# A causal convolution's sums begun two iterations ahead, its pivot at tile 2, and the high parts of the second product ahead of the next silu

## The chip, the cores and the metric

The kernel runs on 1 core of one Trainium2 chip. The metric is device microseconds of one execution: 2212.9 us as the median of 3 runs (2212.4 to 2215.72). One more execution was profiled; all rows below come from it.

The engines are PE (matmuls), DVE and ACT (elementwise work), POOL (elementwise work that may not touch PSUM) and SP, which issues the loads.

## The reference

Two layers over 256 positions of 2048 channels in float32. Only the first sub-layer matters here, the convolution module:

```python
def conv_module(x, pw1_w, pw1_b, dw_w, dw_b, ln_g, ln_b, pw2_w, pw2_b):
    h = x @ pw1_w + pw1_b
    a, gate = jnp.split(h, 2, axis=-1)
    h = a * jax.nn.sigmoid(gate)
    h = lax.conv_general_dilated(...)   # causal, depthwise, width 31
    h = h + dw_b
    h = jax.nn.silu(layer_norm(h, ln_g, ln_b))
    return h @ pw2_w + pw2_b
```

Behind it come a residual with a layer norm, an MLP (2048 to 8192 and back), keys and values, a dilated attention and a second MLP. They are not touched.

## The kernel before

Channels lie on the partitions, so activations are 16 tiles of 128 x 256. Each float32 operand is split into a high part, which PE takes at full rate, and a low part: a product is hi x hi + hi x lo + lo x hi. Weights come in units of 128 x 1024 (`Weights`, L69). Each unit is loaded by SP, cast to its high part by ACT (L117) and reduced to its low part by DVE or POOL (L118). Six high and six low buffers exist, so ACT can cast a unit only when PE has done with the one six back; ACT's casts keep step with PE.

**The convolution module** runs in 16 iterations, one per tile i. PE multiplies the gate half and then the value half of tile i (`pw1`, L247 to L249, 48 matmuls each). ACT takes the sigmoid of the gate (L425). DVE adds the bias to the value half and multiplies (L436, or L433 for tiles 13 and 15): the gated input. DVE then convolves 14 of the tiles itself, one `scalar_tensor_tensor` per tap of width 31 (L482). Its taps are dealt to the iterations by `_plan`, which the change leaves alone. Tiles 13 and 15 are convolved on PE, by matmuls with shifted diagonals (L450), which ACT makes (L420).

A running sum of DVE lies in PSUM. There are three banks (named `o`, `s`, `s`) with two halves each, so six sums. Each tile's first sum starts with its bias: `begin(i)` has ACT write it (L472; L469 for the first tiles). For the layer norm, all tiles are shifted by a pivot, a mean that PE computes from tile 0 (`ln_pivot`, L283, L285). Tiles from `PIVOTED` on get the shift with their bias in `begin`; the earlier ones are shifted afterwards by POOL (L488). `conv_sums` squares a finished tile on ACT (L506) and adds it to two running sums on POOL (L510, L512).

PE and DVE run these iterations in the order in which they are written (`manual_schedule`); ACT and POOL are put in order by the framework's scheduler, which also sets the semaphores.

**The norm and the second product.** `ln_stats` finishes mean and variance. For each tile, DVE multiplies by the scale (L595), ACT takes the silu (L596), ACT casts the high part (L589) and DVE subtracts it for the low part (L590); this runs two tiles behind. PE multiplies with 16 blocks of the second weight (L267, L268), three blocks at once at first, so that each tile is used as it comes. Its last block uses L247 to L249, and the statistics of the next norm begin with L341.

Of the kernel before, what the change touches and what calls it, by code (L numbers as in the profile page):

```python
# [20 lines left out]
T = 256  # L21
D = 2048
KT = D // P
# [31 lines left out]
NGP = 4  # L55
DIAGS = (8192 - NGP * (PAD + T) - 4 * SEG) // 128 * 2
SPLIT = (0, 1, 2, 14)
PIVOTED = 3
STATS_AT = 12

PERIOD, PAIR, STALL, GLU, LATE, SOON = 29, 0.54, 1.34, 2.6, 2, 6
# [69 lines left out]
def trunk(ctx: ExitStack, tc, xt, vecs, dww, dwut, rbt, onehot, w_pw1, w_pw2, w_k, w_v, w_q, w_o, w_1, w_2, out):  # L131
    nc = tc.nc
# [15 lines left out]
    def bank(p, name):  # L148
        return p.tile([P, 512], F32, name=name)
# [130 lines left out]
    def ln_pivot(ln, z0):  # L280

        ps = bank(ps_t, "t")
        nc.tensor.matmul(out=ps[:, 0:T], lhsT=inv, rhs=z0, start=True, stop=True)  # L283
        npiv = small.tile([P, T], F32, name="npiv")
        nc.scalar.mul(out=npiv, in_=ps[:, 0:T], mul=-float(KT))  # L285
        ln["npiv"] = npiv
# [102 lines left out]
    def scale_residual(bias=None, of=range(KT)):  # L389
        for kt in of:  # L390
            y = xres[:, kt, :]
            if bias is None:
                nc.scalar.mul(out=y, in_=y, mul=ALPHA)
            else:
                nc.scalar.activation(out=y, in_=y, func=AF.Identity, scale=ALPHA, bias=vec[:, bias + kt:bias + kt + 1])
# [18 lines left out]
    def make_diags(n):  # L414

        nonlocal made
        for i, g, k in diags[made:min(made + n, taken + DIAGS)]:
            j = made % DIAGS
            with tc.issue_after(W.last_hi.ins):
                nc.scalar.activation(out=work[:, j * 64:(j + 1) * 64], in_=eye, func=AF.Copy, scale=dwu[:, i, g, k:k + 1])  # L420
            made += 1

    def glu(i, a, gate):
        sig = tmp.tile([P, T], F32, name="sig", tag="a")
        on_act = nc.scalar.activation(out=sig, in_=gate, func=AF.Sigmoid,  # L425
                                      bias=vec[:, V_PWB + KT + i:V_PWB + KT + i + 1])
        b = vec[:, V_PWB + i:V_PWB + i + 1]
        if i in PE_TILES:
            ph = ph_of[PE_TILES.index(i) % 2]
            for g in range(2):  # L430
                for s in range(2):
                    h = half(g)
                    nc.vector.scalar_tensor_tensor(out=ph[half(s), g, LAGS - 1:], in0=halves(a)[h, s], scalar=b[h],  # L433
                                                   in1=halves(sig)[h, s], op0=ALU.add, op1=ALU.mult)
        else:
            nc.vector.scalar_tensor_tensor(out=gp_of[DVE_TILES.index(i) % NGP][:, PAD:], in0=a, scalar=b, in1=sig,  # L436
                                           op0=ALU.add, op1=ALU.mult)
        return on_act

    def pe_conv(i, g, midway=None):  # L440

        nonlocal taken
        o = bank(ps_mm, "mm")[:, 0:P]
        ph = ph_of[PE_TILES.index(i) % 2]
        assert taken + 2 * LAGS <= made <= taken + DIAGS and DIAGS % 2 == 0
        for n in range(LAGS):
            if midway and n == STATS_AT:
                midway()
            j = taken % DIAGS
            nc.tensor.matmul(out=o, lhsT=work[:, j * 64:(j + 2) * 64], rhs=ph[:, g, LAGS - 1 - n:LAGS - 1 - n + P],  # L450
                             start=n == 0, stop=n == LAGS - 1)
            taken += 2
        return o
# [10 lines left out]
    def begin(i):  # L464

        if i in DVE_TILES:
            b = vec[:, V_DWB + i:V_DWB + i + 1]
            if i < PIVOTED:
                nc.scalar.activation(out=sum_of[i, 0], in_=inv[:, 0:1].to_broadcast([P, T]), func=AF.Identity, scale=0.0,  # L469
                                     bias=b)  # L470
            else:
                nc.scalar.activation(out=sum_of[i, 0], in_=ln["npiv"], func=AF.Identity, bias=b)  # L472
# [13 lines left out]
    def shift(i):  # L486
        z = conv[:, i, 0:T]
        nc.gpsimd.tensor_tensor(out=z, in0=z, in1=ln["npiv"], op=ALU.add)  # L488
# [16 lines left out]
    def conv_sums(i):  # L505
        nc.scalar.activation(out=conv[:, i, T:2 * T], in_=conv[:, i, 0:T], func=AF.Square)  # L506
        if i >= KT - 2:
            ln["last"].append((conv[:, i, 0:T], conv[:, i, T:2 * T]))
        elif i == 1:
            nc.gpsimd.tensor_tensor(out=ln["acc"], in0=conv[:, 0, :], in1=conv[:, 1, :], op=ALU.add)  # L510
        elif i:
            nc.gpsimd.tensor_tensor(out=ln["acc"], in0=ln["acc"], in1=conv[:, i, :], op=ALU.add)  # L512

    def pw1(units, outs):
        for kt in range(KT):
            h, k = divmod(kt, KT // 2)
            for (_, us), o in zip(units, outs):
                hi, lo = W.get(us[h])
                three(o, hi[:, k * P:(k + 1) * P], lo[:, k * P:(k + 1) * P], x_hl[:, kt, :], kt)

    ended = []

    def pe_convs(at):
        return [(i, g, pe_conv(i, g)) for i, g, when in PE_CONV[:-1] if when == at]

    def pe_ends(convs):
        for i, g, o in convs:
            pe_end(i, g, o)
            if g:
                ended.append(i)  # L530

    def taps(i):
        for *tap, ends in plan[i]:
            dve_tap(*tap, ends)
            if ends == 2:
                if tap[0] < PIVOTED and ln["npiv"] is not None:
                    shift(tap[0])
                ended.append(tap[0])

    begin(0)  # L540
    with tc.manual_schedule(engines={PE, DVE}):
        for i in range(KT):
            if i == 0:
                a, gate = (bank(ps_mm, "mm")[:, 0:T] for _ in range(2))
                pw1(u_pw1[0], (a, gate))
                convs = []
            else:
                acc = bank(ps_mm, "mm")
                a, gate = acc[:, 0:T], acc[:, T:2 * T]
                pw1(u_pw1[2 * i - 1], (gate,))  # L550
                if i == PIVOTED:
                    ln_pivot(ln, conv[:, 0, 0:T])
                    begin(i)
                    for j in ended:
                        shift(j)
                convs = pe_convs(i)
                pw1(u_pw1[2 * i], (a,))
            sigmoid = glu(i, a, gate)
            if i + 1 != PIVOTED:
                begin(i + 1)  # L560
            make_diags(math.ceil((len(diags) - made) / (KT - i)))
            if 4 <= i < 12:
                with tc.issue_after(W.last_hi.ins):
                    scale_residual(V_PW2B, (2 * i - 8, 2 * i - 7))
            pe_ends(convs)
            if i < KT - 1:
                taps(i)
            if i > PIVOTED:
                while ended[:-2] and ended[0] < KT - 2:
                    conv_sums(ended.pop(0))  # L570
        convs = pe_convs(KT)
        taps(KT - 1)
        pe_ends(convs[:-1])
        for j in ended:
            conv_sums(j)
        with tc.issue_after(sigmoid.ins):

            warm = small.tile([P, 1], F32, name="warm")
            nc.scalar.activation(out=warm, in_=inv[:, 0:1], func=AF.Silu)
        i, g, _ = PE_CONV[-1]  # L580
        pe_ends(convs[-1:] + [(i, g, pe_conv(i, g, lambda: ln_early(ln)))])
        conv_sums(KT - 1)
    conv_z = lambda kt: conv[:, kt, 0:T]
    rs = ln_stats(ln, conv_z, 3, u_pw2[0][0][1][0], WARM_C)
    s_hl = act.tile([P, KT, 512], F32R, name="act")

    def split_silu(kt):
        hi, v = s_hl[:, kt, 0:T], conv_z(kt)
        nc.scalar.copy(out=hi, in_=v)  # L589
        nc.vector.tensor_tensor(out=s_hl[:, kt, T:2 * T], in0=v, in1=hi.bitcast(F32), op=ALU.subtract)  # L590

    with tc.manual_schedule(engines={ACT, DVE}):
        for kt in range(KT):
            t = conv_z(kt)
            nc.vector.tensor_tensor(out=t, in0=t, in1=rs, op=ALU.mult)  # L595
            nc.scalar.activation(out=t, in_=t, func=AF.Silu, scale=vec[:, V_CG + kt:V_CG + kt + 1],  # L596
                                 bias=vec[:, V_CB + kt:V_CB + kt + 1])
            if kt >= 2:
                split_silu(kt - 2)
        for kt in (KT - 2, KT - 1):  # L600
            split_silu(kt)


    def residual(units, rhs, first, last, ln, bias=None):
# [81 lines left out]
    for c in range(4):  # L686
        accs = [bank(ps_mm, "mm") for _ in range(2)]
        for kt in range(KT):
            j, k = divmod(kt, 4)
            u = u_v[c][j][k // 2]  # L690
            hi, lo = W.get(u)
            hi, lo = hi[:, (k % 2) * 512:(k % 2 + 1) * 512], lo[:, (k % 2) * 512:(k % 2 + 1) * 512]
# [227 lines left out]
```

## Time and profile before

| what | value |
| --- | --- |
| median of 3 runs | 2212.9 us |
| profiled execution | 2216.65 us |
| its span | 2214.9 us |
| PE busy | 2164.5 us, 98% |
| DVE busy | 1417.5 us, 64% |
| ACT busy | 1037.8 us, 47% |
| POOL busy | 421.7 us, 19% |

The span runs from the first to the last instruction of the profiled execution. A matmul's record lasts longer than the time to the next one, since matmuls are pipelined, so PE counts as busy as long as they follow each other closely. The convolution module, with its second product and the norm behind it, takes roughly the first 360 us. The granted clock of PE has two levels, 1.2 and 2.4 GHz; a mean of 0.80 over a stretch means that part of it ran at the lower one.

### The profile page before, as it was taken

What the parts mean: (1) busy time and instruction counts of PE and PEld (TensorE: products, weight loads), DVE (VectorE), ACT (ScalarE), POOL (GpSimd) and SP (SyncE); (2) the same over time, 40 slices, a digit from 0 to 9 for tenths busy, and PEclk for the clock granted to TensorE, in tenths of its full rate; (3) what the DMA queues carried; (4) which work ended last, traced back from release to release, by engine and by line L of the source; (5) the groups of instructions that cost most, each with busy time, mean ns of one, the idle gap of its engine ahead of it and who ended that gap; (6) DMA issues with size and microseconds to landing.
All of it is one profiled execution on the core that took longest, in us unless ns stands there. A gap on an engine that the chain in (4) does not pass through costs nothing.

```text
span 2214.9 us, 33327 instructions
## 1 busy us (share of the span) xinstructions
PE 2164.5 (98%) x12851; PEld 1909.0 (86%) x12851; DVE 1417.5 (64%) x2218; ACT 1037.8 (47%) x1559; POOL 421.7 (19%) x337
## 2 busy tenths in 40 slices
PE   8997899999999999999999999999999999999997
PEld 8997788888888888888888888878888888888886
DVE  8789567655665665666744476677656656656664
ACT  6664445433543443444644455455434434434443
POOL 5996382000000000015300000640000000000064
PEclk9998899999999999999999999999999999999998
DMA  7553164556855555555465554536555555555552
GB/s 274 185 187 111 46 212 151 189 188 178 249 184 189 185 187 190 190 190 184 136 217 188 192 163 150 189 122 217 187 190 183 188 190 190 190 185 187 186 185 86
DMA packets 113264, 398.04 MB, mean 180 GB/s; under 512 B 12432, under 2 KB 16976, under 8 KB 113104
## 3 DMA queue, kind: packets, MB, share of 16 engines
q1 hardware_dynamic: 111040, 392.75, 53.4%
q10 hardware_dynamic: 2064, 3.15, 1.1%
q8 instruction: 101, 1.65, 0.3%
q14 instruction: 59, 0.48, 0.1%
HBM read 390.61 MB, written 5.24 MB: 179 GB/s over the span
## 4 chain that ended last, share of the span: by engine, by line
PE 92%; DVE 5%; issue 1%; ACT 1%; POOL 1%; DMA 0%; SPq 0%; DVEq 0%; POOLq 0%
PE mm L267 51%; PE mm L268 26%; PE mm L249 3%; PE mm L247 3%; PE mm L248 3%; DVE s L482 2%; PE mm L698 1%; PE mm L696 1%; PE mm L697 1%; DVE o L482 1%; PE mm L450 0%; DMA raw<-in_w_pw 0%; DVE xres L381 0%; POOL act L362 0%; DVE act L368 0%
## 5 line engine op out<-in xcount | busy, mean ns | idle before, releaser
L267 PE MATMUL mm<-act,whi 128*128 128x512 f32 x4928 | 1739.1, 398 | 11.4 <-DVE act L368 5.9
L268 PE MATMUL mm<-act,wlo 128*128 128x256 f32 x4928 | 1383.1, 281 | 1.9 <-POOL wlo L118 1.9
L117 ACT CAST whi<-raw 128x1024 fp32r<-128x1024 f32 (+1 forms) x740 | 770.5, 1045 | 964.0 <-PE mm L267 552.2
L118 DVE TENSOR_TENSOR wlo<-raw,whi 128x1024 fp32r<-128x1024 f32 (+1 forms) x676 | 835.5, 1238 | 590.8 <-ACT whi L117 569.0
L267 PEld LDWEIGHTS mm<-act,whi 128*128 128x128 f32 x4928 | 926.0, 188 | 237.4 <-DVE act L590 8.4
L268 PEld LDWEIGHTS mm<-act,wlo 128*128 128x128 f32 x4928 | 932.6, 189 | 3.5 <-POOL wlo L118 2.2
L618 POOL TENSOR_TENSOR xres<-xres,npiv 128x256 f32<-128x256 f32 x8 | 8.6, 1076 | 1591.2 <-ACT npiv L285 1591.2
L247 PE MATMUL mm<-act,whi 128*128 128x256 f32 x704 | 201.4, 286 | 6.2 <-ACT whi L117 6.2
L249 PE MATMUL mm<-act,wlo 128*128 128x256 f32 x704 | 200.3, 284 | 0.2 <-DVE wlo L118 0.2
L248 PE MATMUL mm<-act,whi 128*128 128x256 f32 x704 | 199.9, 284 | 0.0
L118 POOL TENSOR_TENSOR wlo<-raw,whi 128x1024 fp32r<-128x1024 f32 x64 | 153.0, 2416 | 49.8 <-ACT whi L117 48.3
L247 PEld LDWEIGHTS mm<-act,whi 128*128 128x128 f32 x704 | 135.6, 193 | 7.4 <-ACT whi L117 6.7
L249 PEld LDWEIGHTS mm<-act,wlo 128*128 128x128 f32 x704 | 135.5, 192 | 0.9 <-DVE wlo L118 0.9
L248 PEld LDWEIGHTS mm<-act,whi 128*128 128x128 f32 x704 | 135.7, 193 | 0.1
L482 DVE SCALAR_TENSOR_TENSOR s<-act,dw,s 128x256 f32<-128x256 f32 x266 | 117.6, 482 | 16.7 <-ACT s L472 16.4
L611 DVE TENSOR_TENSOR xres<-mm,xres 128x256 f32<-128x256 f32 x128 | 54.0, 423 | 89.9 <-PE mm L268 73.3
L300 POOL TENSOR_TENSOR ln_acc<-ln_acc,xres 128x256 f32<-128x256 f32 x56 | 80.6, 1440 | 93.5 <-DVE xres L613 93.5
L482 DVE SCALAR_TENSOR_TENSOR o<-act,dw,o 128x256 f32<-128x256 f32 x150 | 72.2, 481 | 2.0 <-ACT o L472 1.4
L613 DVE TENSOR_TENSOR xres<-mm,xres 128x256 f32<-128x256 f32 x156 | 66.1, 424 | 5.1
L296 ACT ACTIVATE sq<-xres 128x256 f32<-128x256 f32 x60 | 25.1, 419 | 80.8 <-DVE xres L613 25.8
L625 POOL TENSOR_TENSOR xres<-xres,npiv 128x256 f32<-128x256 f32 x56 | 56.6, 1039 | 0.0
L234 DVE TENSOR_TENSOR act<-v,act 128x256 fp32r<-128x256 f32 x120 | 50.2, 419 | 6.6 <-ACT act L233 6.6
(146 smaller groups left out, 1120.6 us busy)
## 6 DMA issues: line engine op xcount, KB each, us to landing
raw<-in_w SPq DMA_DIRECT2D x512, 512.0 KB, 4.0
raw<-in_w_pw SPq DMA_DIRECT2D x94, 512.0 KB, 4.0
raw<-in_w_v SPq DMA_DIRECT2D x32, 512.0 KB, 4.3
raw<-in_w_k SPq DMA_DIRECT2D x32, 512.0 KB, 4.4
raw<-in_w_q SPq DMA_DIRECT2D x32, 512.0 KB, 4.3
raw<-in_w_o SPq DMA_DIRECT2D x32, 512.0 KB, 4.4
scratch<-es ACTq DMA_DIRECT2D x1, 3072.0 KB, 35.1
bt<-scratch SPq DMA_DIRECT2D x16, 128.0 KB, 4.1
```

What stands on the lines that cost most here:

```text
L117: self.last_hi = self.nc.scalar.copy(out=hi[:, s], in_=r[:, s])
L118: self.lo_engine[i].tensor_tensor(out=lo[:, s], in0=r[:, s], in1=hi[:, s].bitcast(F32), op=ALU.subtract)
L247: nc.tensor.matmul(out=o, lhsT=hi, rhs=x[:, 0:T], start=kt == 0, stop=False)
L248: nc.tensor.matmul(out=o, lhsT=hi, rhs=x[:, T:2 * T], start=False, stop=False)
L249: nc.tensor.matmul(out=o, lhsT=lo, rhs=x[:, 0:T], start=False, stop=kt == KT - 1)
L267: nc.tensor.matmul(out=acc, lhsT=hi, rhs=x, start=kt == 0, stop=kt == KT - 1)
L268: W.last_mm = nc.tensor.matmul(out=acc[:, T:2 * T], lhsT=lo, rhs=x[:, 0:T], start=False, stop=kt == KT - 1, skip_group_check=True)
L300: nc.gpsimd.tensor_tensor(out=acc[:, 0:T], in0=acc[:, 0:T], in1=z, op=ALU.add)
L482: nc.vector.scalar_tensor_tensor(out=out, in0=tap, scalar=w, in1=o, op0=ALU.mult, op1=ALU.add)
L611: nc.vector.tensor_tensor(out=y, in0=acc[:, 0:T], in1=y, op=ALU.add)
L613: nc.vector.tensor_tensor(out=y, in0=acc[:, T:2 * T], in1=y, op=ALU.add)
L625: nc.gpsimd.tensor_tensor(out=xres[:, b, :], in0=xres[:, b, :], in1=ln["npiv"], op=ALU.add)
```

## The change

Three things change. `PIVOTED` goes from 3 to 2, so PE computes the pivot in iteration 2, and tiles 0 and 1 alone are shifted afterwards. In iteration i the sum of tile i + 2 is begun, where it was that of tile i + 1. A finished tile waits for one more finished tile before its squares are taken. In the silu loop the cast of tile k - 2 (`silu_hi`) is written ahead of the silu of tile k, and the subtraction (`silu_lo`) stays where it was. No instruction of another form is added.

```diff
-PIVOTED = 3
+PIVOTED = 2
...
-    begin(0)
+    for i in range(PIVOTED):
+        begin(i)
...
                 if i == PIVOTED:
                     ln_pivot(ln, conv[:, 0, 0:T])
                     begin(i)
+                    begin(i + 1)
                     for j in ended:
                         shift(j)
...
             sigmoid = glu(i, a, gate)
-            if i + 1 != PIVOTED:
-                begin(i + 1)
+            if i >= PIVOTED:
+                begin(i + 2)
...
             if i > PIVOTED:
-                while ended[:-2] and ended[0] < KT - 2:
+                while ended[:-3] and ended[0] < KT - 2:
                     conv_sums(ended.pop(0))
...
-    def split_silu(kt):
+    def silu_hi(kt):
+        nc.scalar.copy(out=s_hl[:, kt, 0:T], in_=conv_z(kt))
+
+    def silu_lo(kt):
         hi, v = s_hl[:, kt, 0:T], conv_z(kt)
-        nc.scalar.copy(out=hi, in_=v)
         nc.vector.tensor_tensor(out=s_hl[:, kt, T:2 * T], in0=v, in1=hi.bitcast(F32), op=ALU.subtract)
...
         for kt in range(KT):
             t = conv_z(kt)
+            if kt >= 2:
+                silu_hi(kt - 2)
             nc.vector.tensor_tensor(out=t, in0=t, in1=rs, op=ALU.mult)
             nc.scalar.activation(out=t, in_=t, func=AF.Silu, scale=vec[:, V_CG + kt:V_CG + kt + 1],
                                  bias=vec[:, V_CB + kt:V_CB + kt + 1])
             if kt >= 2:
-                split_silu(kt - 2)
+                silu_lo(kt - 2)
         for kt in (KT - 2, KT - 1):
-            split_silu(kt)
+            silu_hi(kt)
+            silu_lo(kt)
```

Line numbers below 540 are the same in both; the silu's lines L589, L590, L595 and L596 of before are L590, L594, L601 and L602 of the changed kernel.

**ACT, iteration 6.** Before: L425 is the sigmoid of tile 6, L117 are casts of weight units, L395 scales the residual, and the last row is the begin of tile 7.

```order
L395 ACTIVATE xres_94<-xres_94,vec_112 128x256
L425 ACTIVATE sig_1486<-mm_1365,vec_112 128x256
L395 ACTIVATE xres_94<-xres_94,vec_112 128x256
L117 CAST whi_1533<-raw_1366 128x1024
L117 CAST whi_1563<-raw_1396 128x1024
L117 CAST whi_1593<-raw_1426 128x1024
L472 ACTIVATE s_191<-npiv_768,vec_112 128x256
```

The same place on ACT now; L472 here is the begin of tile 8.

```order
L117 CAST whi_1456<-raw_1289 128x1024
L420 ACTIVATE act_182<-eye_129,dwu_114 128x64 x8
L395 ACTIVATE xres_94<-xres_94,vec_112 128x256
L425 ACTIVATE sig_1484<-mm_1363,vec_112 128x256
L395 ACTIVATE xres_94<-xres_94,vec_112 128x256
L472 ACTIVATE s_192<-npiv_606,vec_112 128x256
L117 CAST whi_1531<-raw_1364 128x1024
```

The begin of iteration 6 stood three casts behind the sigmoid; it now stands ahead of these casts.

**POOL, the first shift.** Before, from the first low part of a weight unit on POOL; L488 is the shift of tile 0, then of tile 1.

```order
L118 TENSOR_TENSOR wlo<-raw,whi 128x1024 x12
L488 TENSOR_TENSOR act<-act,npiv 128x256
L118 TENSOR_TENSOR wlo<-raw,whi 128x1024 x2
L488 TENSOR_TENSOR act<-act,npiv 128x256
L118 TENSOR_TENSOR wlo<-raw,whi 128x1024
L510 TENSOR_TENSOR ln_acc<-act 128x512
```

The same place on POOL now.

```order
L118 TENSOR_TENSOR wlo<-raw,whi 128x1024 x8
L488 TENSOR_TENSOR act<-act,npiv 128x256
L118 TENSOR_TENSOR wlo<-raw,whi 128x1024 x4
L488 TENSOR_TENSOR act<-act,npiv 128x256
L118 TENSOR_TENSOR wlo<-raw,whi 128x1024 x2
L510 TENSOR_TENSOR ln_acc<-act 128x512
```

Eight low parts instead of twelve stand ahead of the first shift.

**ACT, the silu loop.** Before, from the mean's copy on: L596 is a silu, L589 the cast of the tile two back.

```order
L347 COPY ln_mc<-o 128x256
L596 ACTIVATE act<-act,vec 128x256 x3
L589 CAST act<-act 128x256
L596 ACTIVATE act<-act,vec 128x256
L589 CAST act<-act 128x256
```

The same place on ACT now, with L602 for the silu and L590 for the cast.

```order
L347 COPY ln_mc<-o 128x256
L602 ACTIVATE act<-act,vec 128x256 x2
L590 CAST act<-act 128x256
L602 ACTIVATE act<-act,vec 128x256
L590 CAST act<-act 128x256
```

Each cast moved ahead of one silu; DVE's order in this loop (a multiply, a subtraction two tiles back) is the old one but for two subtractions of weight units that moved out of it.

## Rows read from the trace of the kernel before

**Rows 1.** Windows: busy us (instructions) of each engine, granted clock, DMA share, GB/s.

```profile
180.00:232.00 52.00, 36.04 (x263) 35.58 (x262) 48.21 (x125) 19.35 (x49) 23.18 (x14) 0.80 0.22 74
...
240.00:274.00 34.00, 28.61 (x125) 22.35 (x126) 16.93 (x33) 17.17 (x34) 10.59 (x10) 0.85 0.19 62
...
340.00:360.00 20.00, 16.88 (x95) 13.31 (x96) 15.58 (x32) 8.73 (x17) 10.80 (x14) 1.00 0.14 49
```

**Rows 2.** Waits to 500 us: who waited for whom, us in total, times, longest.

```profile
DVE s L482 <- ACT s L472: 16.4, 4, 7.0
PE mm L450 <- DVE act L433: 16.0, 2, 8.6
...
PE mm L267 <- DVE act L590: 5.2, 8, 2.1
...
ACT s L472 <- DVE s L482: 4.7, 1, 4.7
...
PE mm L268 <- POOL wlo L118: 1.9, 1, 1.9
...
DVE o L482 <- ACT o L472: 1.4, 1, 1.4
```

**Rows 3.** Timeline of DVE: start, us, line, operation, tiles; in brackets idle before.

```profile
39.33 0.42 DVE L484 TENSOR_TENSOR act<-o,act 128x256 f32<-128x256 f32 x1
...
50.24 0.47 DVE L436 SCALAR_TENSOR_TENSOR act<-mm,vec,sig 128x256 f32<-128x256 f32 x1
...
70.29 0.49 DVE L482 SCALAR_TENSOR_TENSOR s<-act,dw,s 128x256 f32<-128x256 f32 x1 [7.04 <-ACT s L472]
...
81.63 0.48 DVE L436 SCALAR_TENSOR_TENSOR act<-mm,vec,sig 128x256 f32<-128x256 f32 x1
...
93.25 0.48 DVE L436 SCALAR_TENSOR_TENSOR act<-mm,vec,sig 128x256 f32<-128x256 f32 x1
...
104.35 0.47 DVE L436 SCALAR_TENSOR_TENSOR act<-mm,vec,sig 128x256 f32<-128x256 f32 x1
```

**Rows 4.** Timeline of PE, from the pivot to the next norm.

```profile
49.90 0.59 PE L283 MATMUL t<-act,inv 128*128 128x256 f32 x2
...
196.10 6.52 PE L450 MATMUL mm<-act 128*128 128x128 f32 x32 [7.37 <-DVE act L433]
...
220.53 8.93 PE L450 MATMUL mm<-act 128*128 128x128 f32 x56 [8.59 <-DVE act L433]
...
239.96 0.50 PE L267 MATMUL mm<-act,whi 128*128 128x512 f32 x1 [2.10 <-DVE act L590]
...
271.08 0.39 PE L267 MATMUL mm<-act,whi 128*128 128x512 f32 x1
...
271.43 0.39 PE L267 MATMUL mm<-act,whi 128*128 128x512 f32 x1
...
344.32 0.61 PE L341 MATMUL mm<-inv,xres 128*128 128x1 f32 x4
```

**Rows 5.** Timeline of ACT in the iterations; the casts are the 37th and the 41st.

```profile
77.32 0.47 ACT L472 ACTIVATE s<-npiv,vec 128x256 f32<-128x256 f32 x1
...
87.89 1.05 ACT L117 CAST whi<-raw 128x1024 fp32r<-128x1024 f32 x1 [1.83 <-PE mm L248]
...
99.41 1.05 ACT L117 CAST whi<-raw 128x1024 fp32r<-128x1024 f32 x1 [1.82 <-PE mm L248]
...
103.05 0.50 ACT L395 ACTIVATE xres<-xres,vec 128x256 f32<-128x256 f32 x1
```

**Rows 6.** Timeline of POOL: the low parts ahead of the first shift.

```profile
28.78 26.12 POOL L118 TENSOR_TENSOR wlo<-raw,whi 128x1024 fp32r<-128x1024 f32 x11 [0.27 <-ACT whi L117]
```

**Rows 7.** Timeline of ACT in the silu loop.

```profile
246.52 0.60 ACT L596 ACTIVATE act<-act,vec 128x256 f32<-128x256 f32 x1 [0.82 <-DVE act L595]
247.03 0.39 ACT L589 CAST act<-act 128x256 fp32r<-128x256 f32 x1
248.24 0.60 ACT L596 ACTIVATE act<-act,vec 128x256 f32<-128x256 f32 x1 [0.83 <-DVE act L595]
```

## The prediction

> **What bounds the kernel now.** I read the windows first, then the waits, then the timelines of DVE, ACT and PE in the stretches that they name. PE is the engine that ends the work, so only time that PE loses counts, and in the first 360 us it loses it in two places. From 180 to 232 us PE is busy 36.04 of 52 us and its granted clock averages 0.80; from 240 to 274 us it is busy 28.61 of 34 at 0.85 [rows 1]. The waits name the causes: PE waited 16.0 us, in two pieces, for L433, DVE's gated input of the two tiles that PE convolves, and 7.1 us (5.2 and 1.9) at the start of the second product for the low parts of the silu (L590) and of a weight unit [rows 2].
>
> Behind the first place stands DVE. It stood idle 17.8 us in five pieces (16.4 and 1.4) for L472, the activation by which ACT starts a sum with its bias [rows 2]; the longest is the 7.04 us ahead of 70.29 [rows 3]. Apart from these pieces DVE works without a gap until the convolution ends, and PE waits for it there at 196.10 (7.37 us) and before 220.53 (8.6 us) [rows 2, 4]. So each microsecond that DVE doesn't idle brings the end of the convolution forward by one, as long as DVE stays behind PE.
>
> **The sums (begin, pivot).** A sum is half a PSUM bank. The tap that waits for L472 is not one of the tile just begun: by the built order it writes the *other* half of that bank, for a tile two or three older. So each begin is a meeting: DVE stops at its next tap on that bank until ACT has come to the begin. Beginning earlier doesn't take the meeting away; it matters where ACT stands by then.
>
> The Trainium skill says in "PSUM — Partial Sum Buffer", section "PSUM bank collisions raise a hardware error", that two engines must be kept apart by bank and quadrant, not by address. By that rule the meeting stays and the term below is 12.3; were the wait by address, all 17.8 would go. The order agrees with the rule.
>
> Where ACT stands I count in casts of weight units (L117), which ACT can only do as PE frees buffers: the 37th at 87.89 and the 41st at 99.41 give 11.52 us for four, one iteration [rows 5]. Up to each begin, before and now: iteration 4, 33 and 33; iteration 5, 39 and 37; 6, 44 and 41; 7, 49 and 46; 8, 53 and 51; 9, 58 and 55. So the meetings come up to three casts (8.6 us) earlier. They also come later in DVE's own row: 2 taps behind the gated input of iterations 4 and 5, then 6, 11, 18 and 23. What is left to wait:
> - Iteration 2. The square of tile 0 stands on ACT ahead of a begin, a cast, eight diagonals, a cast and the sigmoid of tile 2, and waits for tile 0's shift on POOL, now behind 8 low-part subtractions instead of 12. These take 26.12/11 = 2.37 us, so the shift starts at 28.78 + 7 x 2.37 = 45.4 and ends near 46.2 [rows 6]. A cast, eight diagonals, a scaling and a sigmoid took 99.41 to 103.05 = 3.64 us [rows 5]; with the square, the begin and the other cast I estimate 5.0, so the gated input is free to go at 51.3 against 50.24 before [rows 3]: 1.1 us.
> - Iteration 4. DVE would come to its gated input at 81.63 - 7.04 + 1.1 = 75.7 [rows 3], two taps later it is 76.5. The begin stands right behind the 33rd cast, where a begin stood before at 77.32, and ends at 77.8 [rows 5]. Wait 1.3.
> - Iteration 5. 93.25 - 7.04 + 2.4 = 88.6, and two taps: 89.4. The begin stands behind the 37th cast and seven diagonals (1.7, an estimate from the same 3.64): 91.0. Wait 1.6.
> - Iteration 6. 104.35 - 7.04 + 4.0 = 101.3, and six taps of 0.39: 103.7. The begin follows the scaling at 103.05: 103.9. Wait 0.2.
> - From iteration 7 on the begin is three casts ahead of where it was and DVE comes 11 or more taps (4.3 us) later to it: nothing.
>
> That is 4.2 us. The pivot's matmul now asks for tile 0 after the gate of tile 2. PE gets there one iteration before 49.90, at 38.4 [rows 4], and tile 0 is done at 39.33 + 0.42 [rows 3]: PE waits 1.4 us, and the casts with it. With that on the meetings I take 5.5 us: the term is 17.8 - 5.5 = **-12.3**. Its bounds are -17.8 (no meeting waits) and, if ACT falls behind again, 0.
>
> Is DVE still the late one? PE's gate of tile 15 ended at 196.10 - 7.37 = 188.7. With two groups of 32 matmuls at 6.52 (the row, part of it at half clock), half an iteration of 5.76 and the 1.4, PE comes to tile 15's taps at 208.9 at the latest; at full clock, with groups near half as long, near 203. DVE would have its input by 220.53 - 12.3 = 208.2 [rows 4]. So PE still waits, or just doesn't, and the 12.3 holds. The squares a tile later cost nothing: ACT has room between its casts, and the last sums on POOL end ahead of the early statistics. One shift less on POOL is off the path.
>
> **The silu.** A tile took 1.72 us: Silu at 246.52, cast of its high part at 247.03, DVE's subtraction, DVE's multiply for the next tile, next Silu at 248.24 [rows 7]. All four stand in one ring, because the subtraction for tile k-2 comes on DVE ahead of the multiply for k+1 and its cast came behind the Silu of k. With the cast ahead of the Silu the ring spans two tiles: the same 1.72 us for two, 0.86 each. ACT alone needs 0.51 for a Silu and about 0.3 for a cast, 0.8 a tile. PE takes three blocks a tile, each 271.43 - 271.08 = 0.35, so 1.05 [rows 4]. PE becomes the slower one, and the 7.1 us of waits go.
>
> The stage as a check: from PE's first L267 at 239.96 to the last statistics at 344.32 it took 104.4 us [rows 4]. The work is 15 blocks x 16 x 0.35 = 84, a last block of 48 matmuls at 0.12 (11.52 over the 96 of an iteration) = 5.8, and some 2 for pivot and statistics: 92. The other 12 are the 7.1 of waits and the half-clock stretches between them: 0.15 x 34 = 5.1 at most [rows 1]. A dense start leaves no reason for these. I take **-10**, keeping 2 for the first tiles and for casts of later units that stand in ACT's order between the Silus. Bounds: -12.5 and -3 (the rate is hidden behind something else, as the 1.9 for a late weight unit was).
>
> **Sum.** -12.3 - 10 = -22.3. The profiled execution took 2216.65 us (its span 2214.9), so 2194.4; it lies 3.75 above the median of the runs, 2212.9, and I predict 2190.6, say **2191 us**. After the second product the order is the old one.
>
> **The rivals.**
> *The end runs into PE or the clock (0.10).* The new pivot wait could let PE's clock fall to its lower level, 1.2 GHz. For it: idle stretches at 180 to 232 brought the mean to 0.80. Against it: from 340 to 360 PE was busy only 16.88 of 20 us and the clock stayed at 1.00 [rows 1]. If as much ran at half clock as from 240 to 274, 0.15 x 34 / 0.5 = 10 us, PE and all casts would be 5 us late, and of the 12.3 there would be left 7: 2196. The Trainium skill, "TensorE: Matmul & The Clock Gate", Part 1, holds that the clock follows how busy PE has lately been; by that alone a wait of 1.4 us in a dense stretch is small, and the 340 to 360 row agrees.
> *Only one half comes (0.16).* The meetings shift but cost the same: -10, 2203. Or the silu's rate is hidden: -12.3 - 3, 2197.5. The bounds above speak for either.
> *All comes (0.08).* -17.8 - 12.5: 2182.6. Against it: the meetings counted above.
> *Slower (0.05).* ACT works in order. If at the meetings ACT comes first, it is ACT that waits at the begin, and the casts behind it are late. Before, this happened once: 4.7 us [rows 2]. Ten begins at 4.7 are 47 us; PE has a lead of six units of 2.88, 17 us; beyond that it starves: +30, less 10 of the silu, 2233. It decides once ACT's waits pass 17 us in all. Against it: DVE is later than ACT only by the counted taps, and these are short.
> *No change (0.03).* Both gains taken back by waits further on; the rows after 274 us show none that would.
>
> **How the numbers follow.** My forecast has 0.58, with a range of its own of 2186 to 2197. Of the others, the clock (2196), one half (2197.5 to 2203) and a small part of the full gain lie within 2183 to 2203; outside are most of the full gain, no change and slower, 0.16 together with the tails. About 0.2%, 4.4 us, is what a measurement can tell: faster 0.92, within it 0.03, slower 0.05.
>
> **What would show it.** Right: DVE's waits for L472 near 5 us instead of 17.8, the longest under 3; PE no longer waiting at the first convolution on PE and 4 to 6 us at the second; PE's first L267 near 227; no wait of L267 on L590 beyond the first tile, a clock of 1.00 there, and some 94 us to the last statistics. Wrong: ACT waiting on DVE at L472, DVE's waits above 12 us, a half-clock stretch near 40 us, or PE still waiting in every tile of the silu.

## The result and the profile after

Four runs of the changed kernel took 2190.59 us in the median (2190.0 to 2191.53), four of the kernel before, beside them, 2213.05: ratio 0.9897, 95% interval 0.9879 to 0.9914. The prediction was 2191. The profiled execution took 2191.53 (span 2189.7) against 2216.65, so 25.1 less; the medians say 22.5.

First the windows of the kernel after (busy us and instructions of PE, PEld, DVE, ACT and POOL, then clock, DMA share, GB/s). They cover the two places where PE lost time before [rows 1], now earlier in the span, and the next norm's start.

```profile
180.00:220.00 40.00, 35.06 (x280) 34.73 (x279) 36.58 (x95) 18.80 (x49) 23.68 (x13) 0.91 0.34 108
220.00:254.00 34.00, 30.73 (x175) 26.03 (x174) 27.05 (x51) 22.51 (x45) 21.76 (x22) 1.00 0.28 89
...
318.00:338.00 20.00, 16.92 (x94) 13.23 (x93) 15.59 (x35) 9.84 (x20) 10.78 (x14) 1.00 0.16 48
```

In the first place PE stands idle 4.9 of 40 us, where it was 16.0 of 52, and its mean clock has risen from 0.80 to 0.91. In the second one the clock is 1.00. The waits up to 500 us (who waited for whom, us in total, times, longest) answer to [rows 2]:

```profile
PE mm L450 <- DVE act L433: 4.9, 1, 4.9
...
PE mm L267 <- DVE act L594: 3.0, 3, 1.5
...
DVE o L482 <- ACT o L472: 2.8, 1, 2.8
...
DVE s L482 <- ACT s L472: 1.8, 2, 1.5
...
DVE act L436 <- ACT sig L425: 1.0, 1, 1.0
...
PE t L283 <- DVE act L484: 0.7, 1, 0.7
```

DVE waits 4.6 us for the starts of sums (2.8 and 1.8), where it waited 17.8. PE waits once for a gated input, 4.9 us, where it waited twice, 16.0. And PE's 7.1 us at the silu are 3.0. No row is left in which ACT waits for DVE at a start. DVE's timeline (start, us, line, operation; in brackets the idle time before) shows the meetings that are left, against [rows 3]:

```profile
51.75 0.48 DVE L436 SCALAR_TENSOR_TENSOR act<-mm,vec,sig 128x256 f32<-128x256 f32 x1 [1.04 <-ACT sig L425]
...
75.94 0.48 DVE L436 SCALAR_TENSOR_TENSOR act<-mm,vec,sig 128x256 f32<-128x256 f32 x1
...
79.74 0.49 DVE L482 SCALAR_TENSOR_TENSOR o<-act,dw,o 128x256 f32<-128x256 f32 x1 [2.79 <-ACT o L472]
...
92.93 10.28 DVE L482 SCALAR_TENSOR_TENSOR s<-act,dw,s 128x256 f32<-128x256 f32 x26 [1.47 <-ACT s L472]
...
105.85 0.49 DVE L482 SCALAR_TENSOR_TENSOR s<-act,dw,s 128x256 f32<-128x256 f32 x1 [0.29 <-ACT s L472]
```

The meeting before 70.29 that cost 7.04 us is gone. The order also tells what a tap waits for: the one at 79.74 waits for the start of tile 6 (ACT wrote it from 79.24 to 79.71), and the gated input of tile 6 comes only at 103.12. So it is a tap of an older tile, whose sum lies in the other half of that bank. PE's timeline, against [rows 4]:

```profile
190.48 3.74 PE L450 MATMUL mm<-act 128*128 128x128 f32 x32
...
199.80 3.73 PE L450 MATMUL mm<-act 128*128 128x128 f32 x32
...
208.47 8.55 PE L450 MATMUL mm<-act 128*128 128x128 f32 x56 [4.94 <-DVE act L433]
...
226.91 0.50 PE L267 MATMUL mm<-act,whi 128*128 128x512 f32 x1 [1.46 <-DVE act L594]
...
321.15 0.61 PE L341 MATMUL mm<-inv,xres 128*128 128x1 f32 x4
```

At the first tile that PE convolves it waits no more; its groups of 32 matmuls take 3.7 us instead of 6.52, with a granted clock of 1.00 from 190 to 204 us. The second product begins at 226.91 instead of 239.96 (13.05 earlier), and from there to the last statistics it is 94.24 us instead of 104.36 (10.12 less). ACT in the silu loop, against [rows 7]:

```profile
228.98 0.60 ACT L602 ACTIVATE act<-act,vec 128x256 f32<-128x256 f32 x1
229.49 0.39 ACT L590 CAST act<-act 128x256 fp32r<-128x256 f32 x1
229.86 0.60 ACT L602 ACTIVATE act<-act,vec 128x256 f32<-128x256 f32 x1
```

From one silu to the next it is 0.88 us, where it was 1.72.

One caution for what follows. From the last statistics to the end of the span the order of work is the same in all kernels, and yet that part took between 1867.2 and 1870.7 us in the profiled executions: 1870.6 before, 1868.6 in this one, 1867.5 in a later one of the same kernel. Up to 3.5 us of a difference between two single executions are made there by no edit. I therefore compare stages by the first L267 and by the last statistics (the first L341 on the residual) as well, and times by medians. The first L267 scatters too: in the later profile of the changed kernel it comes at 228.97 instead of 226.91, and 1.70 of these 2.06 us are there already at DVE's first gated input (28.24 instead of 26.54). So I also count from that input: from it to the end of DVE's last tap it is 188.8 us in both profiles.

### The profile page after: what moved, and what is told of

The parts are those of the page before. It is cut to its first block, busy times and chain, and to the rows that moved or that the text cites. A ratio compares the mean times of both kernels' runs of the same rounds, so it can differ in the third digit from the quotient of the medians.

```text
span 2189.7 us, 33325 instructions
## 1 busy us (share of the span) xinstructions
PE 2154.9 (98%) x12851; PEld 1902.9 (87%) x12851; DVE 1421.3 (65%) x2218; ACT 1037.8 (47%) x1559; POOL 421.4 (19%) x336
## 4 chain that ended last, share of the span: by engine, by line
PE 90%; DVE 7%; ACT 1%; DMA 1%; issue 0%; SPq 0%; ACTq 0%; DVEq 0%
PE mm L267 52%; PE mm L268 26%; DVE s L482 3%; PE mm L247 2%; PE mm L249 2%; PE mm L248 2%; DVE o L482 2%; PE mm L705 1%; PE mm L703 1%; PE mm L704 1%; PE mm L450 0%; DVE xres L381 0%; DMA xres<-in_xt 0%; DMA raw<-in_w_pw 0%; DVE act L368 0%
## 5 line engine op out<-in xcount | busy, mean ns | idle before, releaser
L267 PE MATMUL mm<-act,whi 128*128 128x512 f32 x4928 | 1733.8, 397 | 8.8 <-DVE act L368 5.9
L117 ACT CAST whi<-raw 128x1024 fp32r<-128x1024 f32 (+1 forms) x740 | 770.7, 1045 | 966.7 <-PE mm L267 554.8
L267 PEld LDWEIGHTS mm<-act,whi 128*128 128x128 f32 x4928 | 924.3, 188 | 231.8 <-DVE act L368 6.2
L625 POOL TENSOR_TENSOR xres<-xres,npiv 128x256 f32<-128x256 f32 x8 | 8.0, 995 | 1582.2 <-ACT npiv L285 1582.2
L296 ACT ACTIVATE sq<-xres 128x256 f32<-128x256 f32 x60 | 25.1, 419 | 77.0 <-DVE xres L620 26.3
L301 POOL TENSOR_TENSOR ln_acc<-ln_acc,sq 128x256 f32<-128x256 f32 x56 | 54.1, 966 | 0.0
```

The source lines that it names most:

```text
L117: self.last_hi = self.nc.scalar.copy(out=hi[:, s], in_=r[:, s])
L267: nc.tensor.matmul(out=acc, lhsT=hi, rhs=x, start=kt == 0, stop=kt == KT - 1)
L301: nc.gpsimd.tensor_tensor(out=acc[:, T:2 * T], in0=acc[:, T:2 * T], in1=sq, op=ALU.add)
```

## The experiments

The expectations call the engines TensorE, VectorE, ScalarE and GpSimd; they are PE, DVE, ACT and POOL. The theory is the prediction's. A start of a sum is a meeting of ACT and DVE at a PSUM bank, each microsecond that DVE loses there moves the convolution's end by one (A); and the silu loop was a ring through ACT and DVE slower than PE (B). The rivals: only one half comes; the meetings are tied to the place of the pivot or of the squares in another way; the wait is not one for the bank.

**Each half alone.** One kernel is the kernel before with the new silu loop and nothing else of the change. The other is the changed kernel with the old loop, in which `split_silu` makes a high part and then its low part:

```
             t = conv_z(kt)
-            if kt >= 2:
-                silu_hi(kt - 2)
...
             if kt >= 2:
-                silu_lo(kt - 2)
+                split_silu(kt - 2)
```

> The kernel before, with the new silu loop alone. Theory (two terms that add: 12.3 us of meetings, 10 us of silu): 2213 - 10 = 2203 us; DVE's waits for L472 stay near 17.8 us, PE's first matmul of the second product stays near 239.5 us of the span, and from there to the last statistics it takes 94 to 95 us instead of 104.4. Rival (the silu's gain needs the earlier end of the convolution, because PE's clock was low there): the stage keeps a half-clock stretch and takes 97 us or more, 2206 us.

> The changed kernel with the old silu loop. Theory: 2213 - 12.3 = 2201 us; DVE waits 5 to 6 us in all on ACT in the iterations, the first matmul of the second product comes near 227.5 us, and the stage from there takes about 104 us as before. Rival (the terms overlap, the earlier start is lost in the silu stage): 2206 us or more with a stage of 108.

The silu's half alone: 2204.17 us (2202.2 to 2206.7), before on that chip 2214.11; ratio 0.9955 (0.9943 to 0.9968), 9.9 us. The convolution's half alone: 2199.49 (2198.46 to 2204.92), ratio 0.9939 (0.9927 to 0.9952), 14.6 us. The sum is 24.5, and the whole change brought 22.5 in the runs above and 23.8 in later ones, so the halves add up and neither pays for the other. In the profiles the first has its first L267 at 239.9 and its last statistics at 334.2: 94.2 us as in the changed kernel, behind an unchanged convolution with 16.3 + 1.4 us of DVE's waits. The second has them at 228.1 and 332.6: 104.5 us, the old stage behind the new convolution. By these marks A is 11.9 and B 10.1; counted from DVE's first gated input (26.16 before, 26.59 here) A is 12.3. The median's 14.6 is no contradiction: its interval reaches from 10.6 to 16.2 us. Of the larger difference between the two profiles, 3.2 us lie in the part whose scatter is told above (1867.4 us here, 1870.6 before).

ACT's timeline in the loop of the convolution's half shows the ring at work (it has the old loop):

```profile
230.67 0.60 ACT L598 ACTIVATE act<-act,vec 128x256 f32<-128x256 f32 x1 [1.36 <-DVE act L597]
231.18 0.39 ACT L591 CAST act<-act 128x256 fp32r<-128x256 f32 x1
232.93 0.60 ACT L598 ACTIVATE act<-act,vec 128x256 f32<-128x256 f32 x1 [1.36 <-DVE act L597]
...
234.65 0.60 ACT L598 ACTIVATE act<-act,vec 128x256 f32<-128x256 f32 x1 [0.82 <-DVE act L597]
```

ACT stands idle ahead of each silu until DVE's product is done. A tile takes 1.72 us, the first ones 2.26: there DVE's subtraction, beside POOL's of 128x256, takes 0.96 us instead of 0.42.

**Is it ACT's order, or the ring?** This kernel gives ACT its old order again and cuts the ring on DVE instead:

```
-            if kt >= 2:
-                silu_hi(kt - 2)
...
             if kt >= 2:
-                silu_lo(kt - 2)
+                silu_hi(kt - 2)
+            if kt >= 3:
+                silu_lo(kt - 3)
+        silu_lo(KT - 3)
```

> The changed kernel, but in the silu loop ScalarE has its old order again (silu of a tile, then the high part of two tiles before), and VectorE's subtraction stands one tile later (three tiles behind its product). Theory (a ring of waits: product, silu, high part, subtraction, next product; any cut through it does): VectorE no longer waits for the high part of the same step, the loop runs at 0.86 to 0.90 us per tile, no TensorE wait on low parts beyond the first tile and the two beside GpSimd's low parts, so 2191 us (2188 to 2194), as the changed kernel. Rival (it is ScalarE's order that counts: the high part must stand ahead of the silu): the loop stays at 1.7 us per tile and the stage at 104 us, about 2200 us, as the kernel with the convolution's edits alone (2199.5).

2192.63 us (2190.45 to 2194.98), ratio 0.99 (0.9887 to 0.9913): the changed kernel's gain, without its order on ACT. Tiles follow each other at 0.88 to 0.89 us here too, and the stage takes 94.2:

```profile
229.38 0.60 ACT L600 ACTIVATE act<-act,vec 128x256 f32<-128x256 f32 x1
229.89 0.39 ACT L590 CAST act<-act 128x256 fp32r<-128x256 f32 x1
230.27 0.60 ACT L600 ACTIVATE act<-act,vec 128x256 f32<-128x256 f32 x1
```

So it is the ring that counted: both cuts through it do the same.

**The pivot a tile later.** The changed kernel with `PIVOTED = 3`, as before:

> The changed kernel with the pivot at tile 3 again, sums still begun two ahead. Theory (what matters is where ACT meets DVE; no begin can stand ahead of the pivot's result): the first meeting, in iteration 3, stays as late as before, some 7 us, and the next comes late too; DVE waits about 11 us on L472 instead of 4.6, so 2190.6 + 6 = 2197 us. Rival (beginning two ahead is what pays, the pivot only saves one shift on POOL): the same as the changed kernel, 2191 us.

2194.33 us (2193.88 to 2194.98), ratio 0.991 (0.9895 to 0.9925). DVE's waits for starts are two:

```profile
70.77 0.49 DVE L482 SCALAR_TENSOR_TENSOR s<-act,dw,s 128x256 f32<-128x256 f32 x1 [6.71 <-ACT s L472]
86.69 0.49 DVE L482 SCALAR_TENSOR_TENSOR o<-act,dw,o 128x256 f32<-128x256 f32 x1 [3.58 <-ACT o L472]
```

That is 10.3 us against 5.6 with the pivot at tile 2 (4.6 for starts, 1.0 for the sigmoid), and the first L267 comes at 231.3, 4.4 later than 226.91 (4.0 counted from the first gated input). DVE's waits come out as end of the convolution, nearly one for one. The time is 3.3 to 3.7 above the two medians of the changed kernel (2190.99 and 2190.59), little more than half of the 6 that I had expected. So the pivot's place is worth a quarter to a third of the convolution's gain, and beginning two ahead, by subtraction, the rest; no run had the pivot at tile 2 and the starts one ahead.

**The squares as before, and three ahead.**

```
-                while ended[:-3] and ended[0] < KT - 2:
+                while ended[:-2] and ended[0] < KT - 2:
```

> The changed kernel, with the squares of a finished tile issued as early as in the kernel before (two tiles kept back instead of three). Theory (the squares were never what VectorE or TensorE waited for; ScalarE is busy 63% of 60 to 180 us): no change, 2191 us (2189 to 2194). Rival (the later squares keep ScalarE free at the meetings, part of the 14.6 us that the convolution's edits brought): VectorE's waits for starts go up from 4.6 us to 7 or more and the time to 2193 to 2197.

2191.13 us (2190.2 to 2193.44), ratio 0.9895 (0.988 to 0.991), beside 2190.99 of the changed kernel on the same chip. The squares a tile later bring nothing that can be measured.

The other kernel begins three ahead (`begin(i + 3)`, with a third start at the pivot). One of its starts, that of tile 5 in iteration 2, overwrites a half to which tile 1's sum is still being added, so its values are not the reference's; the amount of work is the same.

> The changed kernel, with each sum begun three iterations ahead of its taps instead of two. Theory (a start waits for VectorE to leave the other half of its bank, and VectorE for the start; earlier only moves the meeting to another tap, where ScalarE may wait longer): VectorE's waits for starts stay near 5 us, in one or two places, and the time is 2189 to 2195, 2192 taken. Rival (the waits that are left, 2.8 and 1.8 us, are there because two iterations are still too few): both go, 2186 us.

2192.37 us (2192.18 to 2193.33), ratio 0.99 (0.9887 to 0.9912). The waits are fewer and longer, 0.7 and 6.0, and ACT now waits as well:

```profile
DVE o L482 <- ACT o L472: 6.0, 1, 6.0
...
ACT o L472 <- DVE act L484: 2.1, 1, 2.1
```

The rival expected 2186. Earlier doesn't dissolve a meeting, it moves it.

**The start out of PSUM.** That the waiting tap belongs to an older tile is told by the timeline above. If the wait is for the bank, it goes when ACT writes the start into SBUF and DVE's first tap reads it from there:

```
+            start[i] = tmp.tile([P, T], F32, name="begin", tag="de"[i % 2])
-                nc.scalar.activation(out=sum_of[i, 0], in_=ln["npiv"], func=AF.Identity, bias=b)
+                nc.scalar.activation(out=start[i], in_=ln["npiv"], func=AF.Identity, bias=b)
...
-            nc.vector.scalar_tensor_tensor(out=out, in0=tap, scalar=w, in1=o, op0=ALU.mult, op1=ALU.add)
+            nc.vector.scalar_tensor_tensor(out=out, in0=tap, scalar=w, in1=start[i] if first else o, op0=ALU.mult,
+                                           op1=ALU.add)
```

> The changed kernel, but ACT writes a tile's start (bias, or pivot plus bias) to a buffer of its own in SBUF, and DVE's first tap reads it there, so no write of ACT goes into a PSUM bank on which DVE works. Theory (the waits are meetings over a bank): DVE no longer waits on a begin at all, its last tap comes 4 to 5 us earlier; PE hardly waits any more for the input of tile 15. 2186 us if nothing else is late; if the last running sums on POOL, which the early statistics of PE need, become the bound, the gain is given back there: 2190 us with a wait of PE on ln_acc of about 4 us. Rival (ACT is simply late with the start of the tile that is tapped): the same waits of 4.6 us stay, now on the buffer, 2191 us.

2198.84 us (2196.95 to 2199.45), ratio 0.9928 (0.9916 to 0.994): 8 us slower than the changed kernel. Half of the theory held: DVE waits for no start any more, and is busy 119.37 of the 120 us from 60 to 180 (114.81 in the changed kernel). This alone doesn't show that it was the bank: held up by the taps below, DVE comes to the gated input of iteration 4 at 81.21 instead of 75.94, and the start that it met there in the changed kernel had ended at 79.71. ACT now waits at two starts, 2.9 and 1.9 us, for DVE's taps. And the time went into the taps. The groups of DVE up to 235 us (line, names, shapes, count; busy us, mean ns):

```profile
L485 DVE SCALAR_TENSOR_TENSOR s<-act,dw,s 128x256 f32<-128x256 f32 x257 | 113.3, 479 | 0.1
...
L485 DVE SCALAR_TENSOR_TENSOR s<-act,dw,begin 128x256 f32<-128x256 f32 x9 | 12.9, 1437 | 0.1
L485 DVE SCALAR_TENSOR_TENSOR o<-act,dw,begin 128x256 f32<-128x256 f32 x5 | 7.5, 1508 | 0.1
```

The 14 first taps, which read two operands from SBUF, took 20.4 us, 1.46 each instead of 0.48. That is 13.7 us more, for 5.6 of waits saved (the sigmoid's 1.0 went too): 8.1 worse. From the first gated input to the last tap DVE took 196.5 us instead of 188.8, and the first L267 is 8.8 later (235.7). Beside them stands POOL; two of the taps, and what POOL did then:

```profile
81.72 2.52 DVE L485 SCALAR_TENSOR_TENSOR s<-act,dw,begin 128x256 f32<-128x256 f32 x1
...
132.01 0.48 DVE L485 SCALAR_TENSOR_TENSOR s<-act,dw,begin 128x256 f32<-128x256 f32 x1
```

```profile
81.54 2.41 POOL L118 TENSOR_TENSOR wlo<-raw,whi 128x1024 fp32r<-128x1024 f32 x1
...
129.53 2.40 POOL L118 TENSOR_TENSOR wlo<-raw,whi 128x1024 fp32r<-128x1024 f32 x1
132.72 2.41 POOL L118 TENSOR_TENSOR wlo<-raw,whi 128x1024 fp32r<-128x1024 f32 x1 [0.79 <-ACT whi L117]
```

POOL's instruction that began at 81.54 ended at 83.95, and the tap that began at 81.72 ended at 84.24, 0.29 us later. The tap at 132.01 fell into POOL's gap from 131.93 to 132.72 and took 0.48. Four taps took 0.48 to 0.49: three in such gaps, one that came 0.16 us before an end. The other ten took 0.92 to 2.57, and each ended 0.29 us after the end of the POOL instruction that had been running when it came. The Trainium skill states this in "SBUF — State Buffer", section "Who interferes with whom": a VectorE instruction with two SBUF inputs and a GpSimd instruction that reads SBUF exclude each other, and the later one is held until the earlier has ended. These taps agree; I had not weighed it.

**Shorter pieces on POOL.** If a tap is held to the end of one instruction, pieces of half the width should halve the hold. The kernel above, with

```
-        self.lo_engine[i].tensor_tensor(out=lo[:, s], in0=r[:, s], in1=hi[:, s].bitcast(F32), op=ALU.subtract)
+        n = 2 if self.lo_engine[i] is self.nc.gpsimd else 1
+        for k in range(n):
+            c = slice(s.start + k * 1024 // n, s.stop if n == 1 else (k + 1) * 1024 // n)
+            self.lo_engine[i].tensor_tensor(out=lo[:, c], in0=r[:, c], in1=hi[:, c].bitcast(F32), op=ALU.subtract)
```

> The kernel with the start in SBUF (2198.8 us; its 14 first taps of a tile, which read two operands from SBUF beside GpSimd's low parts, took 1.46 us in the mean instead of 0.48), with each of GpSimd's low parts of 128x1024 made in two pieces of 128x512. Theory (such a tap is held until the GpSimd instruction that is running has ended): the most it can wait falls from 2.4 to 1.3 us, the mean of the 14 to 0.9 to 1.1 us, no tap above 1.9; 14 times 0.45 less is 6 us, so 2193 us (2190 to 2197; GpSimd's two pieces together cost perhaps 0.2 us more, and it has some 15 us of waits in that stretch to give). Rival (the form with two operands from SBUF and the result in PSUM is slow by itself, about 1.46 whatever GpSimd does): mean and time as they were, 2199 or more.

A miss, and an instructive one: 2213.31 us in the median of 12 runs that lay between 2190.21 and 2229.37, ratio 0.9971 (0.9945 to 0.9996). Eleven of the 14 first taps took 0.5 to 1.6 us, but three got long, and the mean is 2.69:

```profile
41.27 7.13 DVE L488 SCALAR_TENSOR_TENSOR s<-act,dw,begin 128x256 f32<-128x256 f32 x1
...
108.62 5.62 DVE L488 SCALAR_TENSOR_TENSOR o<-act,dw,begin 128x256 f32<-128x256 f32 x1
...
148.93 14.66 DVE L488 SCALAR_TENSOR_TENSOR o<-act,dw,begin 128x256 f32<-128x256 f32 x1
```

```profile
149.51 1.29 POOL L519 TENSOR_TENSOR ln_acc<-ln_acc,act 128x512 f32<-128x512 f32 x1
150.76 12.53 POOL L121 TENSOR_TENSOR wlo<-raw,whi 128x512 fp32r<-128x512 f32 x10
```

The tap of 14.66 us was held past the instruction that ran when it came and eleven more, and ended at 163.59, 0.29 us after POOL ran out of work (163.30). So "until the instruction that runs has ended" is not enough: with POOL's instructions close behind each other a tap can be passed over many times. Here the measurement goes beyond what the Trainium skill states. All three long taps ended 0.29 us after the last POOL instruction ahead of a gap of POOL (of 2.2, 2.1 and 9.1 us), while eight others got in between two close ones. That there is no semaphore wait between the two halves of a unit doesn't decide it: four of the eight got in just there, and the tap of 14.66 us was passed over at boundaries of either kind. What does decide it isn't settled by these runs. The spread of the 12 runs is what such a chance would look like, but only one of them has a profile.

**The same hold in the changed kernel.** There, DVE's subtraction L594 reads two operands from SBUF, and two of the 16 meet POOL's last low parts:

```profile
236.96 1.94 DVE L594 TENSOR_TENSOR act<-act 128x256 fp32r<-128x256 f32 x1 [1.00 <-ACT act L590]
...
239.16 2.26 DVE L594 TENSOR_TENSOR act<-act 128x256 fp32r<-128x256 f32 x1
```

```profile
236.21 4.92 POOL L118 TENSOR_TENSOR wlo<-raw,whi 128x1024 fp32r<-128x1024 f32 x2 [1.70 <-ACT whi L117]
```

With `TAIL_POOL = 1` instead of 2 DVE makes these two low parts itself:

> The changed kernel, with the two last low parts that GpSimd makes (128x1024, at 236 to 241 us, in the silu loop) made by VectorE instead. Theory (VectorE's subtraction is held while a GpSimd instruction runs): the two subtractions of 1.94 and 2.26 us fall to 0.47; VectorE pays 2 x 1.23 us for the low parts in their place, so the loop ends about 0.8 us earlier and the time is the same or up to 2 us less, 2190 (2187 to 2192). Rival (those two subtractions were slow for another reason, as ScalarE's weight casts beside them): they stay at about 2 us, the low parts come on top, and the time is 2192 to 2194.

> The changed kernel as it is, beside the next one on the same chip: 2191 us (2189 to 2193).

> The changed kernel with GpSimd's two last low parts on VectorE, again, for a comparison on one chip. Theory (the hold of VectorE's subtractions cost TensorE 1.5 us, and its end 2 us): 1.5 to 2.5 us under the changed kernel of this call. Rival (the 1.8 us between the two earlier calls were the chip's): within 0.7 us of it.

First 2188.77 us (2188.01 to 2188.99), ratio 0.9882 (0.9869 to 0.9895); then, beside the changed kernel on one chip, 2189.94 (2188.05 to 2191.79) against 2190.99 (2190.65 to 2192.38), ratios 0.9885 (0.9869 to 0.9902) and 0.9894 (0.9879 to 0.9909). Of this pair on one chip, the first row is L594 in the changed kernel, the second the same with the low parts on DVE (min, median and max ns):

```profile
L594 DVE TENSOR_TENSOR act<-act x16: 413/466/2277, 228.5 to 245.1; 128x256 fp32r<-128x256 f32 x16
```

```profile
L594 DVE TENSOR_TENSOR act<-act x16: 418/461/506, 227.4 to 241.6; 128x256 fp32r<-128x256 f32 x16
```

The hold is gone: no subtraction above 0.51 us, though ACT's order, weight casts included, is unchanged. PE's waits for L594 fall from 3.0 and 2.7 us in the two profiles of the changed kernel to 1.5 in both of this one, and the stage from the first L267 to the last statistics from 94.2 to 92.1 us, twice as well. So the stage lost about 2.1 us by the hold. In time the pair on one chip differs by 1.05 us with overlapping ranges, between what the theory (1.5 to 2.5) and the rival (0.7 at most) had expected: the lowest median here, but not told apart from no change.

## Why the prediction was right

- **That DVE's idle time is the convolution's end, one for one: shown.** DVE lost 12.2 us less (17.8 before; 4.6 and 1.0 now), and from its first gated input to its last tap it took 188.8 us instead of 201.3, 12.4 less. With the pivot at tile 3 it lost 4.7 more than here and took 4.6 longer; three ahead, 1.8 more and 1.8 longer. The second product began 13.05 us earlier in this profile, 11.0 in the later one.
- **That the meetings stay, and where ACT stands decides: shown.** Predicted were 1.1, 1.3, 1.6 and 0.2 us in iterations 2, 4, 5 and 6; measured 1.04, 2.79, 1.47 and 0.29. Three are within 0.15. The one of iteration 4 was mis-sized: its start ended not near 77.8 but at 79.7, because ACT's casts ran 1.9 us later by then (the one ahead of it at 78.28 instead of 76.37). I had put PE's wait at the pivot beside the meetings instead of carrying it into the start. That term in turn was 0.7 and not 1.4. Of the 1.9, 0.97 are there from 16 us on (the same matmul of PE at 16.08 instead of 15.11): ACT's fourth cast had waited 1.07 us for its load instead of 0.05, a difference between two executions. At the pivot 1.2 come to it, the 0.7 among them, and 0.25 go where the pivot stood before. The errors cancel: 5.5 us were taken as left, 5.6 of DVE's are, and that it meets to 0.1 is luck.
- **That the squares cost nothing: shown.** With their old place the time is the same, 2191.13 beside 2190.99.
- **That the silu was a ring: shown, by a cut elsewhere in it.** 0.88 us a tile instead of 1.72, stage 94.24 us where 94 was written down, term -10.1 where -10 was taken. Of it, 4.1 are PE's waits (7.1 to 3.0), and about 5.1 the clock, by the estimate of the prediction (0.15 x 34). Of the waits of PE in it, 3.0 us are left: 1.46 at the first tile, as kept back, and 1.52 at the two subtractions that POOL holds, which I had put down to late casts. With the low parts on DVE the stage takes 92.1, the 92 that the prediction had summed as work.
- **That the clock would not fall in the early stretch: it didn't.** It is 1.00 from 10 to 180 us, the new pivot at 40.19 included, and from 220 us on; the stretch of 180 to 220 at 0.91 has one dip to 0.50, from about 206.0 to 212.8, which begins in PE's one wait of 4.94 us (203.5 to 208.5; predicted 4 to 6).
- **The rivals.** Only one half: refuted by the two halves. All of it: 5.6 us of DVE's waits stay. ACT as the one that waits: not one row in the changed kernel, and 2.1 us when all is begun three ahead. No change and slower: PE's waits further on are as they were (for L368, the largest, 5.9 us in both).

The scale: -22.3 was summed; at the last statistics the two profiles of the changed kernel lie 23.2 and 21.2 us earlier than before (321.15 and 323.12 against 344.32).

## What to carry to other kernels

Where two engines share a guarded bank, count for each of them what stands ahead of the meeting in its own order; starting earlier helps only as far as the slower one's queue really moves, and the next meeting is then the one to count. Find a loop's ring by writing down which instruction on which engine each step waits for: if its length over the tiles that it spans exceeds the consumer's pace, it can be cut by moving one instruction, here in two different places with the same gain. Before a wait is traded for another operand place, look at what else uses that place at the time.

## What was not expected of the hardware

- A VectorE instruction with two operands in SBUF beside a GpSimd one took up to 2.57 us instead of 0.48 when GpSimd's instructions were 2.4 us long, and up to 14.66 us when they were 1.3 us long and followed each other closely. Shorter pieces on GpSimd were worse, not better.
- Such a hold depends on when VectorE comes. Beside GpSimd's subtractions of 128x256, 0.73 us each alone, VectorE's took 0.96 us instead of 0.42 with the old silu loop (at 229.35 and 231.60 in the kernel with the convolution's half alone, each 0.04 us behind the start of one of GpSimd's), but 0.47 in the changed kernel, eight of them at 228 to 235 us, each 0.2 us ahead of an end. GpSimd's own took 0.91 to 0.98 us there.
